# Rotary embedding: ScalarE casts the first f32 rows before it fetches positions and frequencies, and 16 instead of 24 rows of the last tile leave by SyncE's queue

## The chip, the cores and the metric

One core of a Trainium2 chip. The metric is the device time of one execution in microseconds (us). The span of the profile is shorter than this time by some 1.8 us (85.36 against 83.6 for the kernel before). The tensor engine is not used, and the granted clock was 1.00.

## The reference, cut to what matters

```python
# x: (8, 8, 1024, 64) f32, freqs: (32,) f32, positions: (1024,) int
angles = np.outer(positions, freqs)
cos, sin = np.cos(angles), np.sin(angles)
x_first, x_second = x[..., :32], x[..., 32:]
out = concatenate([x_first * cos - x_second * sin,
                   x_first * sin + x_second * cos], axis=-1)      # f32
```

16.8 MB are read and 16.8 MB written. The angles are the same for all 64 heads, so a kernel computes the sines and cosines once and then only multiplies and adds.

## The kernel before

The 64 heads make 8 tiles of 128 partitions x 64 rows x 64 columns. GpSimd loads the tiles (its queue converts f32 to bf16 on the way) and stores the results (bf16 to f32). Two parts are treated apart. The first 16 rows of tile 0 come by SyncE's queue as f32, in two pieces of 256 KB, and ScalarE casts them. The last rows of the last tile are computed into f32 and leave by SyncE's queue, in pieces of 256 KB.

```python
    piece = 8
    head = 2 * piece
    x0 = singles.tile([P, head, d], f32)
    for r in range(0, head, piece):
        nc.sync.dma_start(out=x0[:, r:r + piece], in_=hbm(x, 0, r, r + piece))
    ...
    nc.scalar.dma_start(out=pos_i[0:P:group].bitcast(positions.dtype), in_=...)   # 8 KB
    ...
    nc.scalar.dma_start(out=fr[0:P:32], in_=freqs[None, :].to_broadcast([P // 32, half]))  # 0.5 KB

    for g in range(ntiles):
        lo = 0 if g else head
        nc.gpsimd.dma_start(out=xts[g][:, lo:], in_=hbm(x, g, lo))
    ...                                        # VectorE: spread pos_i and fr over the partitions
    nc.vector.tensor_mul(out=turns, in0=pos_f..., in1=fturn...)
    nc.vector.tensor_scalar(out=whole, in0=turns, ...)         # to the nearest whole turn
    nc.vector.tensor_sub(out=turns, in0=turns, in1=whole)
    nc.scalar.activation(out=sin_h, in_=turns, func=Sin, scale=twopi)
    nc.scalar.activation(out=whole, in_=turns, func=Abs)
    nc.scalar.activation(out=cos_h, in_=whole, func=Sin, scale=-twopi, bias=half_pi)

    nc.scalar.copy(out=xts[0][:, :head], in_=x0)
    ...                                        # rotate: six VectorE products and sums per tile
    tail = 3 * piece
    for g in [1, 0] + list(range(2, ntiles)):
        hi = C if g < ntiles - 1 else C - tail
        ...
        nc.gpsimd.dma_start(out=hbm(out, g, 0, hi), in_=ot)
    last = singles.tile([P, tail, d], f32)
    rotate(ntiles - 1, C - tail, C, last)

    sp = nc.sync
    for done in [pos_i, fr, x0] + ots[:-1]:
        sp.clobber_nop(outs=[sp.lower_ap(done)])      # SyncE waits until these are free
    for r in range(0, tail, piece):
        ...
            sp.dma_start(out=hbm(out, ntiles - 1, lo, lo + piece), in_=last[:, r:r + piece])
```

The scheduler already puts the cast before the sines on ScalarE; the text order above is not the order on the engine. The two fetches stand first there.

## Time and profile before

| | before |
|---|---|
| time, median of 3 | 85.37 us |
| span of the profile | 83.6 us |
| VectorE busy | 63.5 us (76%) |
| transfers | 402 GB/s over the span |
| ScalarE's second f32 piece lands | 11.46 us |
| positions issued, first used by VectorE | 1.03, 4.84 us |
| first product of VectorE starts | 17.13 us |
| VectorE's last result, SyncE's issue of the tail | 73.73, 77.84 us |

VectorE is busy for most of the span, but its last result waits 4.1 us for SyncE, and SyncE waits for stores. An engine that ends early by 4.1 us does not set the end. The lines themselves are in the prediction below, but for SyncE's wait, which is this line of its waits after 70 us (what it waited for: us in total, times, longest us):

```profile
SPq L137 <- DMA out_dram<-ot: 9.6, 2, 4.8
```

### The profile page before, as it was taken

What the parts mean: (1) busy time and instruction counts of PE and PEld (TensorE: products, weight loads), DVE (VectorE), ACT (ScalarE), POOL (GpSimd) and SP (SyncE); (2) the same over time, 40 slices, a digit from 0 to 9 for tenths busy, and PEclk for the clock granted to TensorE, in tenths of its full rate; (3) what the DMA queues carried; (4) which work ended last, traced back from release to release, by engine and by line L of the source; (5) the groups of instructions that cost most, each with busy time, mean ns of one, the idle gap of its engine ahead of it and who ended that gap; (6) DMA issues with size and microseconds to landing.
All of it is one profiled execution on the core that took longest, in us unless ns stands there. A gap on an engine that the chain in (4) does not pass through costs nothing.

```text
span 83.6 us, 163 instructions
## 1 busy us (share of the span) xinstructions
DVE 63.5 (76%) x66; ACT 9.3 (11%) x6; POOL 8.7 (10%) x20
## 2 busy tenths in 40 slices
DVE  1024995089999999999999999999999999920000
ACT  0000049999000000000000000000000000000000
POOL 4960000000002001002002002000100202000000
DMA  0899999999999999999999999999999999999992
GB/s 0 182 202 259 227 208 227 204 227 208 212 220 208 227 208 227 204 212 223 200 388 423 423 455 400 470 388 463 408 439 439 416 455 423 455 392 422 431 331 70
DMA packets 3065, 25.45 MB, mean 304 GB/s; under 512 B 360, under 2 KB 376, under 8 KB 1144
## 3 DMA queue, kind: packets, MB, share of 16 engines
q0 software_dynamic: 2304, 24.12, 94.2%
q1 hardware_dynamic: 720, 1.31, 5.1%
q10 hardware_dynamic: 40, 0.01, 0.0%
q14 instruction: 1, 0.01, 0.0%
HBM read 16.79 MB, written 16.78 MB: 402 GB/s over the span
## 4 chain that ended last, share of the span: by engine, by line
DVE 67%; DMA 12%; ACT 7%; DVEq 1%; SPq 1%; issue 0%; ACTq 0%
DMA x<-in_x_dram 12%; DVE t L114 11%; DVE t L115 11%; DVE ot L119 10%; DVE ot L117 10%; DVE ot L116 10%; DVE ot L118 10%; ACT sin_h L96 2%; ACT L96 2%; ACT L101 2%; ACT xt L101 1%; DVEq L170 1%; DVE last L117 1%; DVE last L118 1%; DVE last L116 1%; SPq L56 1%
## 5 line engine op out<-in xcount | busy, mean ns | idle before, releaser
L114 DVE TENSOR_TENSOR t<-xt,sin_h 128x2048 bf16<-128x2048 bf16 (+2 forms) x9 | 9.9, 1099 | 3.5 <-ACT sin_h L96 3.5
L128 POOL DMA_DIRECT2D out_dram<-ot x8 | 4.2, 526 | 60.4 <-DVE ot L119 60.4
L115 DVE TENSOR_TENSOR t<-xt,sin_h 128x2048 bf16<-128x2048 bf16 (+2 forms) x9 | 9.9, 1099 | 0.0
L117 DVE TENSOR_TENSOR ot<-xt,cos_h 128x2048 bf16<-128x2048 bf16 (+1 forms) x8 | 9.3, 1167 | 0.0
L119 DVE TENSOR_TENSOR ot<-ot,t 128x2048 bf16<-128x2048 bf16 (+1 forms) x8 | 9.3, 1167 | 0.0
L116 DVE TENSOR_TENSOR ot<-xt,cos_h 128x2048 bf16<-128x2048 bf16 (+1 forms) x8 | 9.3, 1166 | 0.0
L118 DVE TENSOR_TENSOR ot<-ot,t 128x2048 bf16<-128x2048 bf16 (+1 forms) x8 | 9.3, 1166 | 0.0
L74 POOL DMA_DIRECT2D xt<-in_x_dram x8 | 4.3, 577 | 0.8 <-PEq L170 0.8
L76 DVE LOAD_MASK_SELECT pos_i<-pos_i x1 | 0.0, 14 | 3.8 <-DMA pos_i<-in_positions_dram 3.8
L101 ACT ACT_TABLE_LOAD x1 | 1.3, 1283 | 11.5 <-DMA x<-in_x_dram 11.5
L87 DVE TENSOR_TENSOR turns<-pos_f,fturn 128x2048 f32<-128x2048 f32 x1 | 2.3, 2293 | 0.0
L93 DVE TENSOR_TENSOR turns<-turns,whole 128x2048 f32<-128x2048 f32 x1 | 2.3, 2293 | 0.0
L99 ACT ACTIVATE cos_h<-whole,half_pi 128x2048 bf16<-128x2048 f32 x1 | 2.0, 2003 | 0.0
L96 ACT ACTIVATE sin_h<-turns 128x2048 bf16<-128x2048 f32 x1 | 1.9, 1909 | 0.0
L98 ACT ACTIVATE whole<-turns 128x2048 f32<-128x2048 f32 x1 | 1.9, 1893 | 0.0
L77 DVE LOAD_MASK_SELECT fr<-fr x1 | 0.0, 14 | 1.9 <-DMA fr<-in_freqs_dram 1.9
L96 ACT ACT_TABLE_LOAD x1 | 1.3, 1283 | 0.0
L91 DVE TENSOR_SCALAR whole<-turns 128x2048 f32<-128x2048 f32 x1 | 1.2, 1226 | 0.0
L101 ACT CAST xt<-x 128x1024 bf16<-128x1024 f32 x1 | 1.0, 1045 | 0.0
L117 DVE TENSOR_TENSOR last<-xt,cos_h 128x768 f32<-128x768 bf16 x1 | 0.9, 950 | 0.0
L119 DVE TENSOR_TENSOR last<-last,t 128x768 f32<-128x768 f32 x1 | 0.9, 950 | 0.0
L116 DVE TENSOR_TENSOR last<-xt,cos_h 128x768 f32<-128x768 bf16 x1 | 0.9, 949 | 0.0
(12 smaller groups left out, 2.6 us busy)
## 6 DMA issues: line engine op xcount, KB each, us to landing
out_dram<-ot POOLq DMA_DIRECT2D x7, 2048.0 KB, 18.5
xt<-in_x_dram POOLq DMA_DIRECT2D x7, 1024.0 KB, 25.2
out_dram<-ot POOLq DMA_DIRECT2D x1, 1280.0 KB, 11.2
xt<-in_x_dram POOLq DMA_DIRECT2D x1, 768.0 KB, 7.6
out_dram<-last SPq DMA_DIRECT2D x3, 256.0 KB, 3.6
x<-in_x_dram SPq DMA_DIRECT2D x2, 256.0 KB, 6.9
pos_i<-in_positions_dram ACTq DMA_DIRECT2D x1, 8.0 KB, 3.7
fr<-in_freqs_dram ACTq DMA_DIRECT2D x1, 0.5 KB
```

The lines of the kernel that those rows point to most:

```text
L74: nc.gpsimd.dma_start(out=xts[g][:, lo:], in_=hbm(x, g, lo))
L87: nc.vector.tensor_mul(out=turns, in0=pos_f.to_broadcast([P, C, half]), in1=fturn.to_broadcast([P, C, half]))
L93: nc.vector.tensor_sub(out=turns, in0=turns, in1=whole)
L96: nc.scalar.activation(out=sin_h, in_=turns, func=Sin, scale=twopi)
L101: nc.scalar.copy(out=xts[0][:, :head], in_=x0)
L114: v.tensor_mul(out=t1, in0=xf, in1=sin)
L115: v.tensor_mul(out=t2, in0=xs, in1=sin)
L116: v.tensor_mul(out=of, in0=xf, in1=cos)
L117: v.tensor_mul(out=os_, in0=xs, in1=cos)
L118: v.tensor_sub(out=of, in0=of, in1=t2)
L119: v.tensor_add(out=os_, in0=os_, in1=t1)
L128: nc.gpsimd.dma_start(out=hbm(out, g, 0, hi), in_=ot)
```

## The change

The intent is to have the cast of the f32 rows first on ScalarE, with the small fetches behind it, and to give GpSimd's last store 48 rows instead of 40, so that less is computed into f32 (slower on VectorE: for 768 columns a step takes 0.87 us into f32 and 0.47 into bf16) and one piece fewer is issued by SyncE.

```diff
+    for g in range(ntiles):
+        lo = 0 if g else head
+        nc.gpsimd.dma_start(out=xts[g][:, lo:], in_=hbm(x, g, lo))
+
+    tc.keep_in_program_order(nc.scalar.copy(out=xts[0][:, :head], in_=x0))
     ...
-    nc.scalar.dma_start(
+    tc.keep_in_program_order(nc.scalar.dma_start(
         out=pos_i[0:P:group].bitcast(positions.dtype),
     ...
-    nc.scalar.dma_start(out=fr[0:P:32], in_=freqs[None, :].to_broadcast([P // 32, half]))
-
-    for g in range(ntiles):
-        lo = 0 if g else head
-        nc.gpsimd.dma_start(out=xts[g][:, lo:], in_=hbm(x, g, lo))
+    tc.keep_in_program_order(
+        nc.scalar.dma_start(out=fr[0:P:32], in_=freqs[None, :].to_broadcast([P // 32, half])))
     ...
-    nc.scalar.copy(out=xts[0][:, :head], in_=x0)
     ...
-    tail = 3 * piece
+    tail = 2 * piece
```

## The prediction

> **What bounds the kernel now.** I read the page's busy shares and slices first, then the chain of waits in order of time, then the SyncE part of the timeline, last the stretches by window.
>
> The slices of the page:
>
> ```profile
> DVE  1024995089999999999999999999999999920000
> DMA  0899999999999999999999999999999999999992
> GB/s 0 182 202 259 227 208 227 204 227 208 212 220 208 227 208 227 204 212 223 200 388 423 423 455 400 470 388 463 408 439 439 416 455 423 455 392 422 431 331 70
> ```
>
> VectorE has a hole in its first fifth and is idle for the last 10 us. The transfers have neither: the queues are full from slice 2 to slice 38. The rate doubles half way because the first half is loads, counted in bf16 bytes written while f32 is read (16.79 MB), and the second half is f32 stores (16.78 MB). So the transfers are the bound, and the chain of waits, which is 67% VectorE, must not be read as "VectorE is the bound".
>
> The head of the chain, in order of time (start us, us, what):
>
> ```profile
> 1.47 9.99 DMA x<-in_x_dram
> 11.46 0.02 issue
> 11.48 0.02 ACTq L101
> 11.50 0.03 issue
> 11.53 1.28 ACT L101
> 12.82 0.01 issue
> 12.83 1.04 ACT xt L101
> 13.87 0.02 issue
> 13.89 1.28 ACT L96
> 15.17 0.01 issue
> 15.18 1.92 ACT sin_h L96
> ```
>
> ScalarE waits for the second f32 piece until 11.46, loads a table, casts, loads the Sin table, and makes the sines; VectorE's main work starts at 17.13. Beside this runs the angle path: positions land at 4.8, frequencies at 7.35, VectorE makes `turns` from 7.35 to 13.66, so the angles are ready 1.5 us before ScalarE asks for them (15.18).
>
> The tail of the timeline (start us, us, engine, line, operation):
>
> ```profile
> 72.78 0.95 DVE L119 TENSOR_TENSOR last<-last,t 128x768 f32<-128x768 f32 x1
> 77.84 2.27 SPq L141 DMA_DIRECT2D out_dram<-last  x3
> ```
>
> VectorE's last result is there at 73.73, SyncE issues it only at 77.84: by the program it first waits for all full tiles to have left. So VectorE is **4.1 us ahead** of the store queue at the end. That slack is the number on which this prediction turns: a delay of VectorE's start up to about 4 us is free, what is beyond it is paid one for one.
>
> **What the Trainium skill says.**
> - "ScalarE: Activation LUTs", What ACT_TABLE_LOAD costs: a switch is about 1283 ns whatever the set. The trace agrees: both loads took 1.28.
> - "VectorE: DVE Perf Modes", Side-by-side for N=2048 bf16: about 1224 ns in the packed mode, 2293 in the plain one. The trace has 1.22 for the bf16 products and 2.29 for `turns`.
> - "DMA: Bandwidth & Descriptors", Queues, rings and completion order: each DMA engine takes turns between the queue rows it has work for. The trace fits: the 256 KB second f32 piece took 9.99 us beside the big loads, the first 3.8 while the queues were still nearly empty (to landing min 3.8, max 10.0).
> - "Perfetto Trace Analysis", DMA Instruction — HWDGE: the profiled window ends when the issuer is free; the movement comes after. So a 0.5 KB fetch is to be priced by its landing: frequencies were issued 1.67 to 2.81 and landed at 7.35, 4.5 us later.
>
> **The change part by part.** The order of instructions of each engine shows that VectorE's and GpSimd's sequences keep their order. On ScalarE, table load and cast stand first, then the two fetches, then the Sin table load and the sines.
>
> 1. *Fetches behind the cast.* ScalarE's sequencer now stands at the wait for the f32 piece (11.46 before), then issues positions, then frequencies. If the issues wait for the table load and cast to end, they start at 13.9; if the sequencer runs on while those execute, at 11.6. No instruction of this trace shows which. Issue of positions 0.60 plus 0.04, of frequencies 0.76 to 1.14 (it was 1.14, perhaps partly behind SyncE's issue): 1.4 to 1.8. Landing after the end of the issue: 4.5 as before, perhaps 3.6 with no f32 piece in the rows: so 5.0 to 6.3 from the start of the issues, middle 5.7.
> 2. *Angles.* Frequencies landed to `turns` done: 13.66 - 7.35 = 6.31. Then the sines 1.92 and two hand-overs, 0.07. The Sin table load is hidden now, as it needs no data. So VectorE's main start = landing + 8.3 (before, ScalarE was the later of the two: 17.13).
>    - run-on: 11.6 + 5.7 + 8.3 = 25.6, a shift of 8.5
>    - issue after the cast: 13.9 + 5.7 + 8.3 = 27.9, a shift of 10.8
> 3. *The f32 piece itself.* Positions and frequencies no longer go into the queues between the first and second f32 piece. They are 8.5 KB, so by bytes nothing changes. But if the second piece stood behind them in the descriptor generator, it lands earlier, by 2 us perhaps (its landing would then follow the first piece's 4.54 by about 4.6 rather than 6.9). I give this 30%.
> 4. *Tail of 16 rows.* VectorE: a bf16 step costs 1.135 at 2048 columns, 0.736 at 1280, 0.47 at 768, hence 0.87 at 1536 and 0.34 at 512; an f32 step 0.87 at 768, about 0.60 at 512. Before 6 x 0.736 + 2 x 0.47 + 4 x 0.87 = 8.84; after 6 x 0.87 + 2 x 0.34 + 4 x 0.60 = 8.30: **0.5 saved**. SyncE issues two pieces rather than three, which takes 0.6 to 0.9 off the end. If the store queue were still the bound, the change would gain up to 0.9.
>
> *Sum.* VectorE ends at 73.73 - 0.53 + S = 73.2 + S with shift S. From the first SyncE issue to the end of the span were 5.76 (83.6 - 77.84); with one piece fewer about 5.1, plus some 0.4 because the last, now larger GpSimd store (1.5 MB, 3.7 us at 430 GB/s) still runs beside it. Span = 78.7 + S, time = span + 1.77 (85.36 - 83.6) = 80.4 + S. This holds where S is over 4 to 5.
>    - run-on, f32 piece unchanged: S 8.5, 88.9
>    - after the cast, unchanged: S 10.8, 91.2
>    - run-on, f32 piece 2.3 earlier: S 6.2, 86.6
>    - after the cast, 2.3 earlier: S 8.5, 88.9
>
> The transfers then run dry near the end: stores start at about 42 and each full one takes 4.9 (2.1 MB at 430), so the seventh could start at 71.5, but VectorE ends that tile at 64.9 + S, over 73.
>
> **The rivals.**
> - *The store queue still hides it*, and the smaller tail wins: 84.5. For it: the queues are full and VectorE idles at the end. Against: the slack is 4.1, and the added path is over twice that unless both helpful readings hold together and the fetches land quickly.
> - *The f32 piece lands earlier*, as its part of the queue is freed: 86 to 87, within 2%. For it: the piece took 10.0 against 3.8 for the first, of equal size. Against: SyncE issued it at 1.47 for 0.58, an issue like its others, and the big loads started at the same time; those explain the slow landing.
> - *Small fetches land far later* in full queues than I took, 7 to 8 us: 93. Against: frequencies already landed among full queues.
>
> **Range and chances.** The four sums have the weights 0.40, 0.30, 0.15 and 0.15, so the middle is near 89.4. The uncertain terms are the start of the issues (2.3), the f32 piece (2.3) and the fetch (0.7 either way): 86.6 to 91.8 holds 8 in 10. Two per cent slower is 87.08. Faster by over 2% would need under 83.66, less than the store queue allows: 0.02. Within 2%: 0.16. Slower: 0.82.
>
> **What would show it right or wrong.** In the new chain the fetch of frequencies must stand between the cast and `turns`, with VectorE waiting for it until 16 to 20 us rather than 7.35. The first product of VectorE should start at 25 to 28 rather than 17.13. The f32 piece's landing (11.5, or near 9) decides part 3; the start of ScalarE's issues against its cast decides run-on. VectorE's tail should be 8.3 from the start of the last tile. SyncE's issue should follow VectorE's last result directly, no longer 4.1 us later, and the transfers should show gaps after 70 us. I am wrong if fetches land within 2 to 3 us of their issue and the f32 piece comes early too, or if VectorE catches up, which I exclude: its products run back to back at fixed lengths.

## The result, and the profile after

The changed kernel is correct and takes **89.46 us** (median of 4, 89.16 to 90.02) against 85.38 for the kernel before in the same rounds. The ratio is 1.0477, with a 95% interval of 1.0411 to 1.0542.

The busy slices of the page of the changed kernel, to be held against those of the kernel before in the prediction:

```profile
DVE  0000000079937999999999999999999999999600
DMA  0999999999999999999999999999896796599992
GB/s 3 191 219 240 238 204 219 212 219 219 212 215 223 204 223 208 219 219 186 409 468 371 468 431 401 475 394 438 345 364 245 297 416 238 238 438 364 407 374 81
```

VectorE (DVE) has next to nothing to do in the first eight slices. Its unbroken row of nines, the products, starts in slice 13 where it started in slice 9 (slices counted from 1), and runs without a pause to its last result; only SyncE's pieces come after that. The transfers (DMA) have gaps from slice 29 on, and the rate falls from some 430 GB/s to between 238 and 438. Before, VectorE's last result had to wait and the queue had no gaps; now it is the reverse. VectorE sets the end.

The chain of waits of the changed kernel, its head in order of time (start us, us, what):

```profile
1.47 10.44 DMA x<-in_x_dram
...
11.98 0.07 ACT L65
12.05 6.02 DMA pos_i<-in_positions_dram
...
22.68 2.30 DVE turns L96
25.01 1.92 ACT sin_h L99
26.95 1.23 DVE t L115
```

The f32 piece lands about where it did (at 11.91, against 11.46). Behind it there now stands a fetch of 8 KB that takes 6.02 us, then the whole angle path of VectorE, then the sines. VectorE's first product starts at 26.95 instead of 17.13: a shift of 9.82 us.

ScalarE's part of the timeline (start us, us, engine, line, operation; ACTq is the engine's sequencer, which issues transfers):

```profile
11.98 1.28 ACT L65 ACT_TABLE_LOAD   x1 [11.98 <-DMA x<-in_x_dram]
12.05 0.60 ACTq L70 DMA_DIRECT2D pos_i<-in_positions_dram  x1
12.69 1.02 ACTq L77 DMA_DIRECT2D fr<-in_freqs_dram  x1
13.28 1.04 ACT L65 CAST xt<-x 128x1024 bf16<-128x1024 f32 x1
14.34 1.28 ACT L99 ACT_TABLE_LOAD   x1
```

The first fetch is issued 0.07 us after the table load begins, and both fetches begin before the cast does. The sequencer was held by the wait for the f32 piece alone. It did not wait for the work it had handed to the engine. So "the fetches come after the cast" is true of the program's order and not of the time: they come after the cast's wait.

The tail of the changed kernel's timeline:

```profile
82.32 0.70 DVE L120 TENSOR_TENSOR last<-last,t 128x512 f32<-128x512 f32 x1
83.05 1.24 SPq L142 DMA_DIRECT2D out_dram<-last  x2
```

VectorE ends at 83.02 and SyncE issues at 83.05. The 4.1 us of slack are gone, and SyncE's last wait before it issues is now for VectorE:

```profile
SPq L142 <- DVE last L120: 1.2, 1, 1.2
```

The busy times by stretch show where the queue runs dry. Columns: stretch, its length, then busy time and instructions of VectorE, ScalarE and GpSimd, the clock, the transfers' busy share, GB/s. Of the changed kernel:

```profile
43.00:62.00 19.00, 19.00 (x17) 0.00 (x0) 1.57 (x3) 1.00 1.05 428
62.00:83.00 21.00, 21.00 (x24) 0.00 (x0) 1.57 (x3) 1.00 0.86 336
```

And of the kernel before, for the late stretch:

```profile
62.00:77.00 15.00, 11.73 (x15) 0.00 (x0) 1.04 (x2) 1.00 1.06 430
```

Until 62 us the stores live on tiles that VectorE had finished while the queue was still busy with loads. A store of a full tile takes 4.9 us (in the packet records of the kernel before, full stores end 4.86 apart) and VectorE needs 6.8 us for one (six products of 1.135), so that stock runs out, and from then on each store waits for its tile.

### The profile page after: what moved, and what is told of

The parts are those of the page before. It is cut to its first block, busy times and chain, and to the rows that moved or that the text cites. A ratio compares the mean times of both kernels' runs of the same rounds, so it can differ in the third digit from the quotient of the medians.

```text
span 88.2 us, 161 instructions
## 1 busy us (share of the span) xinstructions
DVE 62.9 (71%) x66; ACT 9.3 (11%) x6; POOL 8.7 (10%) x20
## 4 chain that ended last, share of the span: by engine, by line
DVE 70%; DMA 19%; ACT 2%; SPq 1%; DVEq 1%; issue 1%; ACTq 0%
DMA x<-in_x_dram 12%; DVE t L115 10%; DVE t L116 10%; DVE ot L118 10%; DVE ot L120 10%; DVE ot L119 10%; DVE ot L117 10%; DMA pos_i<-in_positions_dram 7%; DVE turns L90 3%; DVE turns L96 3%; ACT sin_h L99 2%; DVE whole L94 1%; SPq L56 1%; DVEq L171 1%; DVE last L118 1%; DVE last L117 1%
## 5 line engine op out<-in xcount | busy, mean ns | idle before, releaser
L118 DVE TENSOR_TENSOR last<-xt,cos_h 128x512 f32<-128x512 bf16 x1 | 0.7, 697 | 0.0
L120 DVE TENSOR_TENSOR last<-last,t 128x512 f32<-128x512 f32 x1 | 0.7, 697 | 0.0
L117 DVE TENSOR_TENSOR last<-xt,cos_h 128x512 f32<-128x512 bf16 x1 | 0.7, 696 | 0.0
```

Of the source, the lines that this page charges most:

```text
L117: v.tensor_mul(out=of, in0=xf, in1=cos)
L118: v.tensor_mul(out=os_, in0=xs, in1=cos)
L120: v.tensor_add(out=os_, in0=os_, in1=t1)
```

## The experiments

The theory was: the whole loss is the shift of VectorE's start, less the slack at the end; the shift comes from the fetches being issued behind ScalarE's wait for the f32 piece. The rivals were that the larger last store costs something, that the cast's place costs something by itself, and that VectorE is the bound so that there is no slack. All ten kernels gave correct results. "Shift" is the start of VectorE's first product in the profiled run, less 17.13.

### The tail of 16 rows alone

```diff
 # the kernel before
-    tail = 3 * piece
+    tail = 2 * piece
```

> The kernel before with the tail of 16 rows alone. Theory (the late fetch costs everything, the tail helps a little): the first product of VectorE stays at 17.1, VectorE ends near 73.2, SyncE still issues near 77.8 (it waits for the seventh full store), now two pieces instead of three: 84.5 us, 84.2 to 85.0. Rival A (the larger last store of GpSimd, 1.5 MB, is part of the loss): 86 or more.

Measured: 85.36 us (median of 6 runs), 85.34 before, ratio 1.000 (0.9987 to 1.0013). VectorE's part went as expected: it ended at 72.5, as this run's f32 piece came a little earlier (first product at 16.40). The time did not. SyncE issued two pieces at 77.87, but their landing took longer. The transfers part of the page for the kernel before (KB each, median us from issue to landing):

```profile
out_dram<-last SPq DMA_DIRECT2D x3, 256.0 KB, 3.6
```

And with 16 rows:

```profile
out_dram<-last SPq DMA_DIRECT2D x2, 256.0 KB, 4.3
```

By the trace's packet records, SyncE's first piece begins to move at 79.44 before and at 80.18 here, each time at the moment the first of the 16 engines has done its share of GpSimd's last store. The last packet leaves at 82.34 and at 82.33. The rows taken off SyncE's pieces were put on the store ahead of them. So the expected gain of 0.9 is not there, and nor is rival A's loss: where the queue is the bound, the split is worth nothing either way.

### The new order on ScalarE alone

```diff
 # the changed kernel
-    tail = 2 * piece
+    tail = 3 * piece
```

> The changed kernel with the old tail of 24 rows, so the new order on ScalarE alone. Theory: first product near 27.0 as in the changed kernel, VectorE ends 0.5 later than there (near 83.5), SyncE issues at once, three pieces instead of two: 90.2 us, 89.7 to 91.0, so slower than the changed kernel by 0.5 to 1. Rival A (the tail cost something): at or below 89.2.

Measured: 90.01 us (89.82 to 90.78), ratio 1.0565 (1.0523 to 1.0606). The shift was 9.14 in the profiled run. This is the whole loss and a little more: with VectorE as the bound, the tail of 16 rows is worth having (VectorE's last part is shorter by 0.5, and one issue of 0.6 is saved). The tail thus gains nothing on the old order. On the new one it gains about half a microsecond by the medians (90.01 against 89.46, from different rounds whose ranges overlap: 89.82 to 90.78, 89.16 to 90.02).

### The fetches issued by SyncE

```diff
 # the changed kernel; the cast stays first on ScalarE
-    tc.keep_in_program_order(nc.scalar.dma_start(
+    tc.keep_in_program_order(nc.sync.dma_start(
         out=pos_i[0:P:group].bitcast(positions.dtype),
     ...
-        nc.scalar.dma_start(out=fr[0:P:32], ...
+        nc.sync.dma_start(out=fr[0:P:32], ...
```

> The changed kernel with the two fetches issued by SyncE straight behind the two f32 pieces; the cast stays first on ScalarE, the tail stays 16. Theory (only the issue of the fetches behind ScalarE's wait costs): fetches land by 8 to 12 us, the first product starts at 17.1 to 20.5, a shift of 0 to 3.4, which the slack of 4.1 takes: 84.5 us, 84.2 to 85.2. Rival B (the cast being first costs by itself): 88 or more.

Measured: 85.37 us, ratio 1.0001 (0.9986 to 1.0016), so rival B, at 88 or more, falls. A cost within the slack could not show in the time, but the profile has none: ScalarE had done its cast and its Sin table by 15.19 and waited for `turns` until 19.68. The landing was a miss. From the timeline of this run:

```profile
12.85 0.01 DVE L79 LOAD_MASK_SELECT pos_i<-pos_i  x1 [11.81 <-DMA pos_i<-in_positions_dram]
...
21.62 1.23 DVE L115 TENSOR_TENSOR t<-xt,sin_h 128x2048 bf16<-128x2048 bf16 x1 [1.98 <-ACT sin_h L99]
```

Issued at 2.10, the positions landed 10.7 us later, 1.3 us after the f32 piece that stood ahead of them in the same queue (11.5). The shift was 4.49, not the 0 to 3.4 expected, and it was still free: VectorE ended at 77.69 and SyncE issued at 77.74. This run stands right at the edge of the slack.

### A shorter wait ahead of the fetches

```diff
 # the changed kernel
-    head = 2 * piece
+    head = piece
```

> The changed kernel with 8 f32 rows instead of 16, so ScalarE waits for one piece only, which landed at 4.5 in both kernels. Theory (the length of the wait ahead of the fetches is what counts): fetches issued from 4.6, landed by 10 to 11, first product near 19 to 20, shift 2 to 3, inside the slack: 84.6 us, 84.2 to 85.4. Rival B (cast first costs by itself, whatever it waits for): 88 or more. Rival C (a fetch among full queues takes 6 us wherever it is issued and the rest follows) is told by the landing: 6 after issue would put the first product at 20, still inside the slack.

Measured: 85.33 us, ratio 0.9997 (0.9982 to 1.0011). From its timeline:

```profile
4.75 0.62 ACT L65 CAST xt<-x 128x512 bf16<-128x512 f32 x1 [2.73 <-DMA x<-in_x_dram]
4.76 0.56 ACTq L70 DMA_DIRECT2D pos_i<-in_positions_dram  x1
...
10.36 0.01 DVE L79 LOAD_MASK_SELECT pos_i<-pos_i  x1 [9.31 <-DMA pos_i<-in_positions_dram]
...
19.59 1.22 DVE L115 TENSOR_TENSOR t<-xt,sin_h 128x2048 bf16<-128x2048 bf16 x1 [1.98 <-ACT sin_h L99]
```

The order is that of the changed kernel; the wait for f32 rows is 7 us shorter (with one piece to wait for, the table load is over before it). The fetch still took 5.5 us, and the shift was 2.46, inside the slack. What costs is the length of the wait ahead of the fetches. The fetch is again issued at once beside the cast, and not before it: its own inputs were ready early (the kernel before issued it at 1.03), yet it went out at 4.76, 0.01 us after the cast ahead of it had its data and began.

### The start of VectorE delayed by doses

The product that makes `turns` is repeated. The result does not change, nor does the order on ScalarE.

```diff
 # the kernel before; n is 3, 4 and 6
-    nc.vector.tensor_mul(out=turns, ...)
+    for _ in range(n):
+        nc.vector.tensor_mul(out=turns, ...)
```

> The kernel before with the 2.29 us product for the angles made three times instead of once: VectorE's start is delayed by 2 x 2.26 less the 1.5 by which the angles were early, a shift of 3.0. Nothing else changes. Theory (slack of 4.1 at the end of the store queue): free, 85.2 to 85.8. Rival D (VectorE is the bound, as the chain of waits reads): 88.4.

> The same product made four times: shift 5.3. Theory: 5.3 less the slack of 4.1 is paid, 86.6, 86.0 to 87.2. Rival D: 90.7. Rival E (no slack is lost before the shift is near 8, since stores run faster than VectorE): 85.5.

> The same product made six times: shift 9.8, as in the changed kernel, without its order on ScalarE and with the old tail. Theory: 9.8 less 4.1, 91.1, 90.2 to 91.6, and equal within 0.5 to the new order with the old tail. Rival D: 95.2. If the new order costs something beyond the delay, this run is clearly below that one.

| | shift, us | time, us | ratio (95%) | paid, us | shift less paid |
|---|---|---|---|---|---|
| n = 3 | 3.10 | 85.32 | 0.9993 (0.9966 to 1.0019) | 0 | |
| n = 4 | 5.55 | 86.53 | 1.0141 (1.0117 to 1.0164) | 1.16 | 4.4 |
| n = 6 | 10.10 | 91.10 | 1.0681 (1.0648 to 1.0714) | 5.73 | 4.4 |
| new order, old tail | 9.14 | 90.01 | 1.0565 (1.0523 to 1.0606) | 4.67 | 4.5 |

"Paid" is the median less the median of the kernel before in the same rounds (85.37, and 85.34 for the last row). The zero of the shift, 17.13, is one profiled run; in four runs with the old head the first product starts at 16.40 to 17.55. That moves all the shifts alike and not the slope. A delay of 3.1 is free, and beyond 4.4 each microsecond costs one. Rival D (VectorE the bound) and rival E (slack near 8) are both out. The new order lies on the same line as the mere delay, so it costs nothing but the delay. The tails of the timelines say the same. With n = 6:

```profile
82.88 0.95 DVE L120 TENSOR_TENSOR last<-last,t 128x768 f32<-128x768 f32 x1
83.86 1.89 SPq L142 DMA_DIRECT2D out_dram<-last  x3
```

With the new order and the old tail:

```profile
81.91 0.96 DVE L120 TENSOR_TENSOR last<-last,t 128x768 f32<-128x768 f32 x1
82.90 1.88 SPq L142 DMA_DIRECT2D out_dram<-last  x3
```

SyncE issues 0.96 us apart, and the two profiled runs took 91.03 and 90.07 us, which is 0.96 apart.

### The f32 rows as one transfer

```diff
 # the changed kernel
-    for r in range(0, head, piece):
-        nc.sync.dma_start(out=x0[:, r:r + piece], in_=hbm(x, 0, r, r + piece))
+    nc.sync.dma_start(out=x0, in_=hbm(x, 0, 0, head))
```

> The changed kernel with the 16 f32 rows loaded as one transfer of 512 KB instead of two of 256 KB. Theory F (the second piece is slow because it reaches the queues after the big loads): one transfer issued first lands whole by 5 to 6.5 us, fetches land by 12, first product near 20 to 21, shift near 3.5: 84.4 to 85.5. Rival G (512 KB beside the big loads take 10 us however they are issued): landing near 11, 89 us.

Measured: 85.47 us, ratio 1.0015 (0.9988 to 1.0042). The 512 KB landed 5.5 us after their issue at 0.74, where of two transfers of half the size the second landed at 10.7 to 11.9 us. The fetches were issued at 6.24, positions landed 5.7 us later, and the first product started at 21.19, a shift of 4.06. Theory F held, and the packet records show how. In the kernel before, the first piece moves from 2.19 to 3.82, GpSimd's first load begins at 3.50, and the second piece (issued at 1.47) moves only from 5.34 to 10.42, among the loads. Here all 512 KB move from 2.17 to 5.36. The packets are of 4 KB here and of 2 KB there, but that is not the gain: nearly alone, 256 KB took 1.6 us and 512 KB took 3.2. Whether the second piece comes late by its time of issue or as the second of its queue is not told apart. That is one edit that makes the changed kernel as fast as the kernel before.

### Can both kernels be beaten at the tail?

As the split was worth nothing, I tried to let SyncE issue its pieces as soon as VectorE is done, with 16 and with 24 rows.

```diff
 # the kernel before, with tail = 2 * piece or 3 * piece
-    for done in [pos_i, fr, x0] + ots[:-1]:
+    for done in [pos_i, fr, x0] + ots[:5]:
         sp.clobber_nop(outs=[sp.lower_ap(done)])
     ...                                       # the issue of the last pieces
-    sp.clobber_nop(outs=[sp.lower_ap(ots[-1])])
+    for done in ots[5:]:
+        sp.clobber_nop(outs=[sp.lower_ap(done)])
```

> The kernel before with the tail of 16 rows, and SyncE no longer waits for the seventh full store before it issues the two last pieces (it collects that wait, and the eighth's, afterwards). Theory H (the tail of 16 gained nothing alone because the last pieces move only when the last GpSimd store has run off its engines, at some 270 GB/s instead of 430): issued at 73.2, as soon as VectorE is done, the pieces share the queues with the stores and the end comes when all bytes are out at full rate: 84.5 us, 84.2 to 84.9. Rival I (the end is fixed by bytes at any order): 85.3.

> The same early issue with the old tail of 24 rows. Theory H: bytes count, not how they are split, so within 0.3 of the run with 16 rows: 84.5. Rival J (16 rows are better once the issue is early): 0.5 slower than it.

Measured: 85.28 us, ratio 0.9987 (0.9967 to 1.0007), and 85.35 us, ratio 0.9995 (0.9977 to 1.0013). Theory H falls and rival I holds. With 16 rows the pieces were issued at 73.16, 4.7 us earlier than before, and only their landing grew:

```profile
out_dram<-last SPq DMA_DIRECT2D x2, 256.0 KB, 8.9
```

By the packet records the first of them moved at 79.65, some 0.6 us before the first engine was done with its share of GpSimd's last store, and the last packet left at 82.32. In the run with 24 rows the times are 79.44 and 82.32. So in four kernels with different splits and different times of issue, the last packet left at 82.32 to 82.34. The queues are not full to there. In the last whole microsecond the transfers' busy share is 0.63 to 0.82 in the four kernels, as here for the kernel before and for the early issue with 16 rows:

```profile
81.00:82.00 1.00, 0.00 (x0) 0.00 (x0) 0.00 (x0) 1.00 0.82 260
81.00:82.00 1.00, 0.00 (x0) 0.00 (x0) 0.00 (x0) 1.00 0.67 244
```

That the end does not move is shown; that it could not is not: theory H's full rate up to the last byte was never reached. Why pieces issued at 73.16 move only when the stores ahead are all but gone is not settled by these runs. No version tried here beats the kernel before.

## Why the prediction was right or wrong

**The bound and the slack: right.** The prediction read the slack of 4.1 us off the tail of the timeline and said that a delay up to about that is free and the rest is paid one for one. The doses gave 4.4 and a slope of one. (Part of the 0.3 between them is that SyncE's pieces end sooner when VectorE is last: 5.3 to 5.4 us from the first issue to the end of the span with n = 4 and n = 6, 5.76 in the kernel before.) The sum "time = 80.4 + S" gives 90.2 for the profiled run's shift of 9.82, and that run took 90.02. Its term from SyncE's issue to the end, 5.1 + 0.4, measured 5.15 (83.05 to 88.2).

**Issue behind the wait, part 1: right in kind, one branch decided, one term too small.** The prediction left open whether the issues wait for the cast. They do not; the trace has them 0.07 us after the table load's start. It counted 5.0 to 6.3 us, middle 5.7, from the start of the issues to the use of the frequencies. It was 6.6: issue at 12.05, the frequencies spread from 18.66. The term that was mis-sized is the landing after the end of the issues: 3.6 to 4.5 were counted. In the three variants in which VectorE waited for the frequencies (the new order with the old tail, 8 f32 rows, one f32 transfer) it was 4.9 to 5.0, and 6.5 to 6.7 from the start of the issues. In the changed kernel's own profile the sign that the prediction named, VectorE waiting for the frequencies, is missing: it waited for the positions, which landed at 18.07, and when it had spread and cast them the frequencies were there. They still arrived last: in the packet records their last packet leaves at 18.00, that of the positions at 17.10. So the order of the fetches was right, and only the size was off. The third rival's 7 to 8 us were not reached.

**The branch sum.** For "run-on, f32 piece unchanged" the prediction had S of 8.5 and 88.9 us. The shift was 9.82: the piece landed 0.5 later than in the trace before, and the fetches took 0.9 more. The prediction averaged this branch with a slower one that did not occur, and this made up for the fetch that was too short. So its 89.4 met the measured 89.46 partly by luck: the timed runs spread from 89.16 to 90.02, while the kernel before spreads by 0.3 in these rounds. The weights as stated give 89.2 and not 89.4, and 78.7 + 1.77 is 80.5 rather than 80.4; neither changes the argument.

**The f32 piece, part 3: the likelier side was right.** It landed at 11.91 with the fetches gone from ahead of it, 11.26 with the old tail, against 10.7 to 11.9 in the kernels that kept the old order. The 30% for an earlier landing were not earned.

**The tail, part 4: VectorE's term right, the queue's term wrong.** VectorE took 8.38 us for the last tile (74.64 to 83.02) where 8.30 were computed. The statement "if the store queue were still the bound, the change would gain up to 0.9" failed: alone, the tail gained 0.0, since SyncE's pieces move after GpSimd's last store and the bytes of both are the same in sum. By this, the first rival's 84.5 was out of reach too: the three variants with the new order and the small tail whose shift stayed within the slack took 85.33 to 85.47.

**Where the queue runs dry: right, but too late.** "Gaps after 70 us" came from 62 us on. The prediction followed the seventh store alone; with 6.8 us for a tile against 4.9 for a store, the queue had caught up two tiles earlier.

**The rivals.** "The store queue still hides it" became true in the three variants whose shift stayed at 2.5 to 4.5 (fetches by SyncE, 8 f32 rows, one f32 transfer), and not in the change itself.

## What to carry to other kernels

A small fetch that starts a long chain must not stand in an engine's queue behind a wait for a large transfer: it costs its own landing again, among full queues, after the wait (6.0 us for 8 KB here). Before pricing a delay, look at the end of the trace for how long the delayed engine's last result waits; that much is free, and the rest is paid one for one. Where the transfers are the bound, moving rows or issues between queues may change which of them is last and not when, as it did in four kernels here.

## What the Trainium skill lacked or had wrong

- "DMA: Bandwidth & Descriptors", Latency and other measured facts: it has a first byte after some 0.6 us for SyncE's and ScalarE's queues and no landing time for a small transfer among full queues. Here the first packet of the first f32 piece moved 1.45 us after its issue began at 0.74, with nothing ahead of it. The 8 KB of positions took 3.3 to 3.9 us to land when issued at 1.03, 5.5 to 6.0 when issued among full queues, and 10.7 behind an f32 piece of the same queue.
- "DMA: Bandwidth & Descriptors", Queues, rings and completion order: each engine is said to take turns between the queue rows with work, packet by packet. While loads run the records agree: the second f32 piece moves among GpSimd's loads from 5.34 to 10.42 in the kernel before. While stores run they did not: in the run with the early issue and 16 rows, pieces that SyncE issued at 73.16, with two GpSimd stores already queued, did not move until 79.65, with 0.6 us to go until the first engine had done its share of the last of them (80.25). None moved at 76.45 to 77.31 either, where the engines ended their shares of the first of the two stores. Turns were not to be seen over those 6.5 us; the cause stays open.
- No page prices a transfer by what is ahead of it and beside it in the queues: 512 KB issued first landed in 5.5 us, while a second piece of 256 KB, issued 0.7 us after a first one, took 9.3 to 10.4.
